# Layer 1's projections for two heads ahead of the heads' small products, exponentials among the raw weights, and the ring of weights one place on

## The chip, the cores and the metric

The kernel runs on one core of a Trainium2 chip. The metric is the device time of one execution in microseconds (us). The core has four engines that matter here: TensorE (PE in the profile, with its weight loads as PEld), VectorE (DVE), ScalarE (ACT) and GpSimd (POOL). SyncE (SP) issues the transfers from HBM. Each engine works through its own list of instructions in order; semaphores tie the lists together.

## The reference

The kernel computes a trunk of two layers over 512 tokens of width 1024, in float32. Layer 0 mixes tokens with four heads of differential attention and four groups of trailing means. Layer 1 is gated linear attention with four heads. Each layer ends with an MLP of width 4096 with squared ReLU. Layer 1, cut to what the change touches:

```python
def _gla_mixer(h, w_in, w_gk_up, b_gk, norm_gain, w_out):     # h is the normed input, chunks of 64 tokens
    proj = h @ w_in                        # q 512, k 512, v 1024, g_out 1024, gk_low 16
    log_a = log_sigmoid(gk_low @ w_gk_up + b_gk) / 16.0        # one decay per token and key channel
    ...
    b = cumsum(gi)                                             # within a chunk
    o_inter = einsum('bhlk,bhkv->bhlv', qi * exp(b), state)
    decay = exp(where(causal, b_i - b_j, -inf))
    attn = einsum('bhijk,bhjk->bhij', qi * decay, ki)
    o_intra = einsum('bhij,bhjv->bhiv', attn, vi)
    new_state = exp(b_last) * state + einsum('bhlk,bhlv->bhkv', ki * exp(b_last - b), vi)
    ...
    o = _rmsnorm(o, norm_gain) * silu(g_out)
    return o @ w_out
```

## The kernel before

Activations lie channel by channel: eight tiles of [128 channels x 512 tokens]. A float32 product is made of three matmuls, since both factors are split into a high and a low part: high weight by high activation (L148), high by low (L149), low by high (L150). A projection into channel-major form (`proj_T`) takes 24 such matmuls into one PSUM bank; a projection into token-major form (`proj_tok`, L172 to L174) takes 96 into four banks at once.

**Banks.** PSUM has eight banks under two names, four "mm" (in the profile `psmm`) for the large products and four "ax" (`psax`) for small products, sums and transposes. A tile takes a name's banks in turn, and waits until the bank's last reader is done.

**Weights.** They arrive in pieces of 1 MB by SP's queue (`load`, L115) into a ring of raw slots (`wraw`), two slots outside the MLPs and five within. Slot k is columns 4Sk to 4S(k+1) of one raw buffer of 24 S columns (S is 512). Each half of a slot is split by ScalarE into the high part (L126, `wh`) and by VectorE into the low part (L127, `wl`), with four tiles each in turn. The very first piece goes in parts straight to slot 0 (`raw0`). Where only two slots are in use, the other columns of the raw buffer serve as spare tiles of 512 columns, `spare(k)`.

**The start.** The norm of a layer is applied after the projection: while PE projects, the squares of x are summed (L246), PE adds them over the partitions (L204 and L205), ScalarE and VectorE form the inverse root, the row `rb` (L216, L217, L209 to L211), and an eviction multiplies a bank by `rb` on its way out (L311 for layer 0's q and k).

**Layer 1.** Head 0's q and k are projected first; then the gates of all four heads run through ScalarE (L697, L698, logarithm L706) and VectorE (subtraction L712, scan L713). `weights(h)` projects a head's q and k (but not head 0's), evicts them (L731 and L735), and makes the head's weights: exponentials of the scans (L722), three transposes (L753), the sums of q·k by chunk (L204, L205), products of 64, 32 and 16 columns (L783), and larger ones (L790), each of them between steps on VectorE and ScalarE. These are called a head's small products here. `values1(i)` projects half of the values in token-major form. `outputs(h)` makes a head's states and outputs (L825, L840, L842), their squares (L844, L848) and the norm of the head (L204, L205, L216, L217, L209). Behind them come the gate projections from `wg1`, Silu on them (L877), and the output projection from `wo1`.

**The order.** The program is written once, and a scheduler at build time orders each engine's list by priority: what is written earlier goes earlier where its inputs allow, `soon()` raises the priority of what stands in it, and `issue_after` holds an instruction behind another. ScalarE holds one set of functions at a time; a change of set is an instruction of its own, ACT_TABLE_LOAD.

Of the kernel before, what the change touches and what calls it, by code (L numbers as in the profile page):

```python
# [13 lines left out]
ALU = mybir.AluOpType  # L14
AX = mybir.AxisListType

P = 128
# [18 lines left out]
def trunk(ctx: ExitStack, tc: tile.TileContext, xT, par, lvl, lam4, wqk0, wu0, wv0, poolw, wo0,  # L36
          wgk, wup, wqk1, wv1, wg1, wo1, w1a, w2a, w1b, w2b, gfin, out):
    nc = tc.nc
    V, A, G, PE = nc.vector, nc.scalar, nc.gpsimd, nc.tensor
# [4 lines left out]
    def T(shape, tag, bufs, dt=F32):  # L44
        cnt[0] += 1
        return sb.tile(shape, dt, tag=tag, bufs=bufs, name=f"{tag}_{cnt[0]}")
# [6 lines left out]
    def turn(name, bufs):  # L53
        ring[name] = ring.get(name, -1) + 1
        return ring[name] % bufs
# [4 lines left out]
    row8 = row16 = tmp2 = row  # L60


    def spare(k):
        return raws[:, k * S:(k + 1) * S]
# [16 lines left out]
    def PS(tag, shape=(P, S)):  # L81
        cnt[0] += 1
        return pp.tile(list(shape), F32, tag=tag, bufs=4, name=f"ps{tag}_{cnt[0]}")

    def small(n, tag="sm"):
        return T([P, n], tag, 24)


    def soon(n=300):
        return tc.high_priority(n)  # L90
# [3 lines left out]
    nc.scalar.dma_start(prm[:, 0:C_ICNT], par[:, 0:C_ICNT])  # L94
    xall = T([P, KB, S], "x", 1)
    x = [xall[:, f, :] for f in range(KB)]
    raw0 = raws[:, 0:4 * S].rearrange("p (a n) -> p a n", a=2)
    xT3 = xT.rearrange("(f p) s -> p f s", p=P)
    for f, nx, nw in ((0, 1, 1), (1, 1, 1), (2, 2, 2), (4, 2, 4), (6, 2, 0)):
# [46 lines left out]
    def mm3(ps, w, a, first, last):  # L146
        (wh, wl), (ah, al) = w, a
        PE.matmul(ps, wh, ah, start=first, stop=False)  # L148
        PE.matmul(ps, wh, al, start=False, stop=False)  # L149
        ended["mm"] = PE.matmul(ps, wl, ah, start=False, stop=last).ins  # L150

    def proj_T(w, act, tag="mm", ps=None, kbs=tuple(range(KB)), first=0, last=KB - 1):

        hi, lo = w
        ps = PS(tag) if ps is None else ps
        for kb in kbs:
            c = slice(kb * P, (kb + 1) * P)
            mm3(ps, (hi[:, c], lo[:, c]), act[kb], kb == first, kb == last)
        return ps
# [106 lines left out]
    act = []  # L266
# [13 lines left out]
    st = Stream(wqk0, 2)  # L280
# [4 lines left out]
    with tc.issue_after(ended["hi"]), tc.issue_after(ended["lo"]), tc.issue_after(ended["mm"]):  # L285
        rb = nrm.rb()
# [19 lines left out]
    def qk_heads(h):  # L306
        for j in range(2):
            ps = (ps0, ps1)[h][j] if h < 2 else proj_T(st.next(), act)
            t = spare(8 + 2 * h + j)
            with soon():  # L310
                V.tensor_tensor(t, ps, rb, ALU.mult)  # L311
            qk[h, j] = t
# [22 lines left out]
    def softmax(h, qt, views, neg):  # L335

        n = (qt + 1) * P
        es, rs, sums, c2 = [], small(2), small(2), small(1)
        for j in range(2):
            e = tmp2()  # L340
            A.activation(e[:, :n], views[j], AF.Exp, bias=neg[:, j:j + 1], scale=0.125, accum_out=sums[:, j:j + 1])
            es.append(e)
        V.reciprocal(rs, sums)
        V.tensor_tensor(c2, rs[:, 1:2], neglam, ALU.mult)
        V.tensor_scalar(out=es[1][:, :n], in0=es[1][:, :n], scalar1=c2, scalar2=None, op0=ALU.mult)
        V.scalar_tensor_tensor(out=es[0][:, :n], in0=es[0][:, :n], scalar=rs[:, 0:1], in1=es[1][:, :n],
                               op0=ALU.mult, op1=ALU.add)
        return es[0]
# [52 lines left out]
    st = Stream(wu0)  # L401
    for i, g in enumerate((3, 2, 1, 0)):
        w = POOL_W[g]
        ps = proj_T(st.next(), act)
# [5 lines left out]
        while step < w:  # L410
# [7 lines left out]
                               op1=ALU.subtract)  # L418
# [234 lines left out]
    act, nrm = add_out(wo0, cat, C_FFN0, NH - 1)  # L653
# [8 lines left out]
    act, nrm = ffn(w1a, w2a, act, nrm, C_MIX1)  # L662
# [4 lines left out]
    st = Stream(wqk1)  # L667
# [11 lines left out]
    with soon():  # L679
        rb = nrm.rb()  # L680
# [6 lines left out]
    qT0, kT0 = row8(), row8()  # L687
# [3 lines left out]
    es, ms, bs = [], [], []  # L691
    for h in range(NH):
# [3 lines left out]
        e, m = tmp(), tmp2()  # L696
# [23 lines left out]
    def expo(out, src):  # L720
        with tc.issue_after(exps):
            last_exp[0] = A.activation(out, src, AF.Exp, scale=GT).ins  # L722

    def weights(h):

        qT, kT = qT0, kT0
        if h:
            ps = proj_T(st.next(), act)
            qT = row8()
            with soon():  # L730
                V.scalar_tensor_tensor(out=qT, in0=ps, scalar=float(P) ** -0.5, in1=rb, op0=ALU.mult, op1=ALU.mult)  # L731
            ps = proj_T(st.next(), act)
            kT = row8()
            with soon():
                V.tensor_tensor(kT, ps, rb, ALU.mult)  # L735
        b = bs[h]
        b3 = b.rearrange("p (c t) -> p c t", t=P)

        e = row16()
        expo(e, b)  # L740
        el = small(NT)
        V.tensor_copy(el, e.rearrange("p (c t) -> p c t", t=P)[:, :, P - 1])
        ebl.append(el)
        V.tensor_tensor(e, e, qT, ALU.mult)
        qeb.append(e)
        d = tmp()
        d3 = d.rearrange("p (c t) -> p c t", t=P)
        V.tensor_tensor(d3, b3[:, :, P - 1:P].to_broadcast([P, NT, P]), b3, ALU.subtract)
        expo(d, d)
        V.tensor_tensor(d, d, kT, ALU.mult)  # L750
        pst = PS("ax")
        for c in range(NT - 1):
            PE.transpose(pst[:, c * P:(c + 1) * P], d[:, c * P:(c + 1) * P], ident)  # L753
        kd = row16(3 * P)
        A.activation(kd, pst[:, 0:3 * P], AF.Copy)
        kdt.append(kd)

        at = row16()
        at3 = at.rearrange("p (c t) -> p c t", t=P)
        attn.append(at)  # L760
        prod = tmp()
        V.tensor_tensor(prod, kT, qT, ALU.mult)
        V.tensor_tensor(at3, col_sums(prod, 0.0).rearrange("p (c t) -> p c t", t=P),
                        lv[:, NLEV:NLEV + 1, :].to_broadcast([P, NT, P]), ALU.mult)
        for l in range(NLEV - 1):
            s = 64 >> l
            nb = S // (2 * s)
            sh = [P, nb, s]
            d = tmp()
            bv, dv, kv, qv = (t.rearrange("p (n t) -> p n t", t=2 * s) for t in (b, d, kT, qT))  # L770
            ref = bv[:, :, s - 1:s].to_broadcast(sh)
            V.tensor_tensor(dv[:, :, 0:s], ref, bv[:, :, 0:s], ALU.subtract)
            V.tensor_tensor(dv[:, :, s:], bv[:, :, s:], ref, ALU.subtract)
            expo(d, d)
            V.tensor_tensor(dv[:, :, 0:s], dv[:, :, 0:s], kv[:, :, 0:s], ALU.mult)
            V.tensor_tensor(dv[:, :, s:], dv[:, :, s:], qv[:, :, s:], ALU.mult)
            psl = PS("ax")
            if s >= 16:

                for p0 in range(0, P, 2 * s):  # L780
                    for c in range(NT):
                        j0 = c * P + p0
                        PE.matmul(psl[p0:p0 + s, c * s:(c + 1) * s], d[:, j0:j0 + s], d[:, j0 + s:j0 + 2 * s],  # L783
                                  start=True, stop=True)
                    A.activation(at3[p0:p0 + s, :, p0 + s:p0 + 2 * s],
                                 psl[p0:p0 + s, 0:NT * s].rearrange("p (c t) -> p c t", t=s), AF.Copy)
                continue
            for c in range(NT):
                cs = slice(c * P, (c + 1) * P)
                PE.matmul(psl[:, cs], d[:, cs], d[:, cs], start=True, stop=True)  # L790
            V.copy_predicated(at3, lv[:, l:l + 1, :].to_broadcast([P, NT, P]),
                              psl.rearrange("p (c t) -> p c t", t=P))

        d = tmp(S // 2)
        bv, kv, qv = (t.rearrange("p (n t) -> p n t", t=2) for t in (b, kT, qT))
        V.tensor_tensor(d, bv[:, :, 1], bv[:, :, 0], ALU.subtract)
        expo(d, d)
        V.tensor_tensor(d, d, kv[:, :, 0], ALU.mult)
        V.tensor_tensor(d, d, qv[:, :, 1], ALU.mult)
        pair = [P, NT, P // 2, 2]  # L800
        V.copy_predicated(at.rearrange("p (c n t) -> p c n t", c=NT, t=2),
                          lv[:, NLEV - 1:NLEV, :].rearrange("p a (n t) -> p a n t", t=2).to_broadcast(pair),
                          col_sums(d, 0.0).rearrange("p (c n t) -> p c n t", c=NT, t=1).to_broadcast(pair))
# [5 lines left out]
    def values1(half):  # L809
        for t, ps in enumerate(proj_tok(vst, act)):  # L810
            vt = spare(12 + 4 * half + t)
            with soon():
                A.activation(vt, ps, AF.Copy, scale=r1[:, t:t + 1])
            vv[t][half] = vt
# [39 lines left out]
            ot.append(o)  # L854


    for h in range(3):
        weights(h)
    values1(0)
    weights(3)  # L860
    outputs(0)
    outputs(1)
    values1(1)
    outputs(2)
    outputs(3)

    st = Stream(wg1)
    gts = []
    for f in range(KB):
        ps = proj_T(st.next(), act)  # L870
# [12 lines left out]
    act, nrm = add_out(wo1, oh, C_FFN1, KB - 1)  # L883
# [86 lines left out]
```

## Time and profile before

| | |
|---|---|
| median of 3 runs | 1117.22 us (1116.67 to 1118.0) |
| profiled execution | 1116.72 us |
| its span (first to last instruction) | 1114.8 us |
| mean granted clock of TensorE | 0.983 |
| TensorE busy | 1078.9 us, 97% |
| VectorE busy | 827.7 us, 74% |
| ScalarE busy | 532.4 us, 48% |
| moved from HBM | 100.59 MB |

A row of the timeline gives the start, the duration, engine, line, operation, output <- inputs, and in brackets how long the engine had been idle and what released it. A row of the windows gives the stretch, its length, the busy time and number of instructions of PE, PEld, DVE, ACT and POOL, the granted clock of PE, the busy share of DMA and GB/s. A row of the page's groups gives a count, the total busy time and the mean of one in ns, then the idle time ahead of it. Line numbers are those of the kernel before; in the changed one they are higher by 1 from the new `turn` on and by up to 9 towards the end.

### The profile page before, as it was taken

To read this page: it belongs to the slowest core of one execution; us is meant where nothing else is said; L and a number is where in the kernel's file an instruction comes from. 1 tells how busy PE (TensorE), PEld (TensorE's weight loads), DVE (VectorE), ACT (ScalarE), POOL (GpSimd) and SP (SyncE) were. 2 spreads that over 40 slices of the span, in tenths; PEclk is the share of its full clock that TensorE was granted. 3 is DMA by queue.
4 is the path that set the end of the run, shared out by engine and by line. 5 is a ranking of instruction groups with operands and counts; after the bars stand their busy time and mean duration, and the time that the engine had idled before them with its cause. 6 is when DMAs were issued, how large, how long until landed. Compare 5 with 4: busy or idle time off the path is not lost.

```text
span 1114.8 us, 12893 instructions
## 1 busy us (share of the span) xinstructions
PE 1078.9 (97%) x4968; PEld 869.2 (78%) x4968; DVE 827.7 (74%) x1234; ACT 532.4 (48%) x885; POOL 2.3 (0%) x20
## 2 busy tenths in 40 slices
PE   7999969999999999999969999999999999999996
PEld 5676748888888888888757778888888888888885
DVE  6757667696497597598888877655697596696696
ACT  6444525455454453454554546544553443453453
POOL 0000000000000000000000000000000000000000
PEclk9999979999999999999979999999999999999999
DMA  7132123214304305203220222342305305206102
GB/s 239 73 113 82 71 85 124 85 38 151 118 34 170 130 4 189 76 17 114 76 76 1 76 76 77 113 151 86 123 1 189 113 1 195 108 1 223 41 1 76
DMA packets 17917, 103.52 MB, mean 93 GB/s; under 512 B 2016, under 2 KB 3040, under 8 KB 6208
## 3 DMA queue, kind: packets, MB, share of 16 engines
q1 hardware_dynamic: 17712, 102.67, 25.6%
q8 instruction: 39, 0.64, 0.2%
q14 instruction: 22, 0.18, 0.1%
q10 hardware_dynamic: 144, 0.03, 0.0%
HBM read 100.59 MB, written 2.10 MB: 92 GB/s over the span
## 4 chain that ended last, share of the span: by engine, by line
PE 92%; DVE 4%; ACT 2%; DMA 1%; issue 1%; SPq 0%; DVEq 0%
PE psmm L148 14%; PE psmm L149 14%; PE psmm L150 14%; PE psmm L566 6%; PE psmm L565 6%; PE psmm L567 6%; PE psax L148 3%; PE psax L150 3%; PE psax L149 3%; PE psax L567 3%; PE psax L565 3%; PE psax L566 3%; PE psmm L174 2%; PE psmm L173 2%; PE psmm L172 2%; PE psax L325 1%
## 5 line engine op out<-in xcount | busy, mean ns | idle before, releaser
L126 ACT ACTIVATE wh<-wraw 128x1024 fp32r<-128x1024 f32 x230 | 243.5, 1061 | 403.0 <-PE psmm L149 161.6
L127 DVE TENSOR_TENSOR wl<-wraw,wh 128x1024 fp32r<-128x1024 f32 x230 | 280.8, 1222 | 64.8 <-ACT wh L126 63.9
L148 PE MATMUL psmm<-row,wh 128*128 128x512 f32 x736 | 290.6, 396 | 15.3 <-DVE wraw L408 7.2
L149 PE MATMUL psmm<-row,wh 128*128 128x512 f32 x736 | 291.1, 396 | 0.4 <-DVE row L187 0.4
L150 PE MATMUL psmm<-row,wl 128*128 128x512 f32 x736 | 290.4, 395 | 0.0
L148 PEld LDWEIGHTS psmm<-row,wh 128*128 128x128 f32 x736 | 139.2, 189 | 48.7 <-DVE wraw L408 7.8
L149 PEld LDWEIGHTS psmm<-row,wh 128*128 128x128 f32 x736 | 139.4, 189 | 32.6 <-issue 3.1
L150 PEld LDWEIGHTS psmm<-row,wl 128*128 128x128 f32 x736 | 139.3, 189 | 31.2 <-issue 2.6
L565 PE MATMUL psmm<-wh,row 128*128 128x512 f32 x320 | 124.6, 390 | 0.0
L567 PE MATMUL psmm<-wl,row 128*128 128x512 f32 x320 | 124.6, 389 | 0.0
L566 PE MATMUL psmm<-wh,row 128*128 128x512 f32 x320 | 124.6, 389 | 0.0
L540 DVE TENSOR_TENSOR wraw<-wraw 128x1024 f32<-128x1024 f32 x64 | 77.4, 1222 | 0.3
L492 DVE TENSOR_TENSOR row<-row,row 128x512 fp32r<-128x512 f32 x112 | 75.1, 685 | 0.3 <-ACT row L491 0.3
L567 PEld LDWEIGHTS psmm<-wl,row 128*128 128x128 f32 x320 | 60.1, 188 | 12.5
L566 PEld LDWEIGHTS psmm<-wh,row 128*128 128x128 f32 x320 | 60.1, 188 | 12.4
L565 PEld LDWEIGHTS psmm<-wh,row 128*128 128x128 f32 x320 | 60.1, 188 | 12.4
L491 ACT ACTIVATE row<-row 128x512 fp32r<-128x512 f32 x112 | 65.7, 618 | 5.3 <-DVE row L518 5.3
L506 DVE SCALAR_TENSOR_TENSOR tmp<-psmm,rb 128x512 f32<-128x512 f32 x48 | 33.0, 687 | 45.7 <-PE psmm L150 45.7
L511 ACT ACTIVATE row<-tmp 128x256 f32<-128x256 f32 x128 | 45.9, 406 | 11.0 <-DVE tmp L506 10.7
L150 PE MATMUL psax<-row,wl 128*128 128x512 f32 x128 | 49.8, 389 | 0.0
L567 PE MATMUL psax<-wl,row 128*128 128x512 f32 x128 | 49.8, 389 | 0.0
L149 PE MATMUL psax<-row,wh 128*128 128x512 f32 x128 | 49.8, 389 | 0.0
(233 smaller groups left out, 1316.5 us busy)
## 6 DMA issues: line engine op xcount, KB each, us to landing
wraw<-in_w1a SPq DMA_DIRECT2D x16, 1024.0 KB, 4.8
wraw<-in_w2a SPq DMA_DIRECT2D x16, 1024.0 KB, 4.8
wraw<-in_w1b SPq DMA_DIRECT2D x16, 1024.0 KB, 4.8
wraw<-in_w2b SPq DMA_DIRECT2D x16, 1024.0 KB, 4.8
wraw<-in_wo SPq DMA_DIRECT2D x8, 1024.0 KB, 4.7
wraw<-in_wqk SPq DMA_DIRECT2D x7, 1024.0 KB, 4.8
wraw<-in_wv SPq DMA_DIRECT2D x6, 1024.0 KB, 4.8
wraw<-in_wg SPq DMA_DIRECT2D x4, 1024.0 KB, 4.7
```

The lines of the kernel that those rows point to most:

```text
L126: ended["hi"] = A.activation(hi, src, AF.Copy).ins
L127: ended["lo"] = V.tensor_tensor(lo, src, hi.bitcast(F32), ALU.subtract).ins
L148: PE.matmul(ps, wh, ah, start=first, stop=False)
L149: PE.matmul(ps, wh, al, start=False, stop=False)
L150: ended["mm"] = PE.matmul(ps, wl, ah, start=False, stop=last).ins
L491: A.activation(hi, src, AF.Copy)
L492: V.tensor_tensor(lo, src, hi.bitcast(F32), ALU.subtract)
L511: A.activation(raw[name][:, j, :], r[:, th * 256:th * 256 + 256], AF.Square)
L540: V.tensor_tensor(out[k], in0[k], in1[k], ALU.subtract)
L565: PE.matmul(ps[t], hi, wh[:, cs], start=f, stop=False, skip_group_check=True)
L566: PE.matmul(ps[t], lo, wh[:, cs], start=False, stop=False, skip_group_check=True)
L567: PE.matmul(ps[t], hi, wl[:, cs], start=False, stop=l, skip_group_check=True)
```

## The change

There are three edits. First, the ring of raw slots is turned one place on ahead of the first load, so that the second piece of `wqk0` goes to slot 1 and not to slot 0, in which `raw0` lies. Every later piece outside the MLPs lies in the other slot of the two. Second, layer 0's q and k tiles use four spare tiles in turn (8 to 11), and the softmax's exponentials `e`, which came from the pool of rows, now use four others (12 to 15). Third, in layer 1 q and k of a head are projected by a function of its own, `project()`, which is called for heads 1 and 2 before `weights(0)`; the calls that follow are values, weights and projections in turn, and the four outputs come last.

```diff
     x = [xall[:, f, :] for f in range(KB)]
+    turn("raw", 2)
     raw0 = raws[:, 0:4 * S].rearrange("p (a n) -> p a n", a=2)
...
-            t = spare(8 + 2 * h + j)
+            t = spare(8 + 2 * (h % 2) + j)
...
-            e = tmp2()
+            e = spare(12 + turn("es", 4))
             A.activation(e[:, :n], views[j], AF.Exp, bias=neg[:, j:j + 1], scale=0.125, accum_out=sums[:, j:j + 1])
...
+    qks = [(qT0, kT0)]
+
+    def project():
+
+        ps = proj_T(st.next(), act)
+        qT, kT = row8(), row8()
+        with soon():
+            V.scalar_tensor_tensor(out=qT, in0=ps, scalar=float(P) ** -0.5, in1=rb, op0=ALU.mult, op1=ALU.mult)
+        ps = proj_T(st.next(), act)
+        with soon():
+            V.tensor_tensor(kT, ps, rb, ALU.mult)
+        qks.append((qT, kT))
+
     def weights(h):
 
-        qT, kT = qT0, kT0
-        if h:
-            ps = proj_T(st.next(), act)
-            qT = row8()
-            with soon():
-                V.scalar_tensor_tensor(out=qT, in0=ps, scalar=float(P) ** -0.5, in1=rb, op0=ALU.mult, op1=ALU.mult)
-            ps = proj_T(st.next(), act)
-            kT = row8()
-            with soon():
-                V.tensor_tensor(kT, ps, rb, ALU.mult)
+        qT, kT = qks[h]
...
-    for h in range(3):
-        weights(h)
+    project()
+    project()
+    weights(0)
     values1(0)
+    weights(1)
+    project()
+    weights(2)
+    values1(1)
     weights(3)
     outputs(0)
     outputs(1)
-    values1(1)
     outputs(2)
     outputs(3)
```

The lists of instructions move at three places. The first is SP's queue at the start, from the last of the first small transfers on (`in_par` are parameters, `in_lam` a small vector of the attention). Before:

```order
L103 DMA par_62<-in_par 128x192
L115 DMA wraw_61<-in_wv 128x2048
L115 DMA wraw_61<-in_wqk 128x2048
L292 DMA tmp_282<-in_lam 128x256
L115 DMA wraw_61<-in_wv 128x2048
L115 DMA wraw_61<-in_wqk 128x2048 x2
```

Now:

```order
L104 DMA par_62<-in_par 128x192
L116 DMA wraw_61<-in_wqk 128x2048
L116 DMA wraw_61<-in_wv 128x2048 x2
L293 DMA tmp_282<-in_lam 128x256
L116 DMA wraw_61<-in_wqk 128x2048 x2
```

The load of `wqk` stands first, and the first load of `wv` behind it.

The second place is VectorE in layer 1, from the last scans of the gates (L713, now L714) to the start of head 0's chain. Before, and here 29 instructions of head 0's chain and one correction of its sums lie between the two pieces:

```order
L713 SCALAR_TENSOR_TENSOR row_4279<-row_3999,row_4256 128x512
L713 SCALAR_TENSOR_TENSOR row_4282<-row_3999,row_4263 128x512
L748 TENSOR_TENSOR tmp_4297<-row_4273 128x512
L742 COPY sm_4294<-row_4292 128x4
L127 TENSOR_TENSOR wl_4874<-wraw_61,wh_4873 128x1024
L744 TENSOR_TENSOR row_4292<-row_4292,row_4235 128x512
```

```order
L798 TENSOR_TENSOR tmp_4410<-tmp_4410,row_4236 128x256
L799 TENSOR_TENSOR tmp_4410<-tmp_4410,row_4235 128x256
L791 COPY_PREDICATED row_4307<-lvl_1586,psax_4392 128x512
L731 SCALAR_TENSOR_TENSOR row_4453<-psmm_4428,rb_4216 128x512
L735 TENSOR_TENSOR row_4484<-psmm_4459,rb_4216 128x512
```

Now:

```order
L714 SCALAR_TENSOR_TENSOR row_4241<-row_3967,row_4210 128x512
L128 TENSOR_TENSOR wl_4580<-wraw_61,wh_4579 128x1024
L714 SCALAR_TENSOR_TENSOR row_4244<-row_3967,row_4217 128x512
L713 TENSOR_TENSOR row_4224<-row_4224,tmp_4223 128x512
L713 TENSOR_TENSOR row_4231<-row_4231,row_4230 128x512
L714 SCALAR_TENSOR_TENSOR row_4247<-row_3967,row_4224 128x512
L714 SCALAR_TENSOR_TENSOR row_4250<-row_3967,row_4231 128x512
L732 SCALAR_TENSOR_TENSOR row_4290<-psmm_4265,rb_4184 128x512
L735 TENSOR_TENSOR row_4291<-psmm_4297,rb_4184 128x512
L732 SCALAR_TENSOR_TENSOR row_4353<-psmm_4328,rb_4184 128x512
L735 TENSOR_TENSOR row_4354<-psmm_4360,rb_4184 128x512
L753 TENSOR_TENSOR tmp_4391<-row_4241 128x512
```

The four evictions of the projections (L732 and L735) stand right behind the scans, and a weight split (L128) among the scans. On ScalarE, the weight splits move in the same way: the one of `wh_4550` stands ahead of the gates' second and third exponential, and the one of `wh_4579` between the second and third logarithm. On PE, the last matmul of head 2's k projection had head 0's transposes (L753) right behind it; now 23 matmuls of the value projection stand between the two.

The third place is ScalarE at the outputs: Silu (L877, now L886), the inverse root of a head's norm (L216 and L217, now L217 and L218), and squares of outputs (L844, L848, now L849, L853). Before:

```order
L216 ACTIVATE tmp_5383<-psax_5384 128x512
L217 ACTIVATE tmp_5383<-tmp_5383 128x512
L844 ACTIVATE tmp_5416<-psax_5408 128x512
L848 ACTIVATE row_5418<-psax_5408,par_62 128x512
L844 ACTIVATE row_5428<-psax_5420 128x512
L848 ACTIVATE row_5430<-psax_5420,par_62 128x512
L126 ACTIVATE wh_5572<-wraw_61 128x1024
L202 ACTIVATE row_5435<-tmp_5416 128x512
L877 ACT_TABLE_LOAD
L877 ACTIVATE wraw_61<-wraw_61 128x512
L216 ACT_TABLE_LOAD
L216 ACTIVATE tmp_5433<-psax_5434 128x512
```

Now:

```order
L886 ACT_TABLE_LOAD
L886 ACTIVATE wraw_61<-wraw_61 128x512
L849 ACTIVATE row_5296<-psax_5288 128x512
L853 ACTIVATE row_5298<-psax_5288,par_62 128x512
L127 ACTIVATE wh_5601<-wraw_61 128x1024
L886 ACTIVATE wraw_61<-wraw_61 128x512
L203 ACTIVATE row_5303<-tmp_5284 128x512
L886 ACTIVATE wraw_61<-wraw_61 128x512
L217 ACT_TABLE_LOAD
L217 ACTIVATE tmp_5301<-psax_5302 128x512
L218 ACT_TABLE_LOAD
L218 ACTIVATE tmp_5301<-tmp_5301 128x512
```

Silu was met first behind the third output's norm; now it is met ahead of it, and the table is changed before each following norm. ScalarE's list had 8 ACT_TABLE_LOADs and now has 13.

## The prediction

> **What bounds the kernel now.** I read the page's span, its busy shares and the chain of waits first, then the waits of PE, then PE in stretches of time, then the timeline where a stretch is not full.
>
> ```profile
> span 1114.8 us, 12893 instructions
> PE 1078.9 (97%) x4968; PEld 869.2 (78%) x4968; DVE 827.7 (74%) x1234; ACT 532.4 (48%) x885; POOL 2.3 (0%) x20
> PE 92%; DVE 4%; ACT 2%; DMA 1%; issue 1%; SPq 0%; DVEq 0%
> ```
>
> PE is busy for 97% of the span and carries 92% of the chain that ends last, so only a place where PE waits, or runs at a lower clock, can give time back. Such places are few:
>
> ```profile
> 0.00:20.00 20.00, 14.08 (x48) 9.60 (x48) 12.85 (x27) 13.49 (x28) 0.40 (x7) 1.00 0.82 273
> 20.00:40.00 20.00, 18.17 (x75) 13.69 (x76) 15.05 (x32) 8.28 (x13) 0.00 (x0) 0.91 0.34 115
> 40.00:140.00 100.00, 99.17 (x418) 69.21 (x416) 65.63 (x173) 50.22 (x137) 0.56 (x5) 1.00 0.24 83
> 140.00:160.00 20.00, 11.65 (x30) 6.89 (x31) 13.46 (x26) 4.85 (x8) 0.67 (x6) 0.66 0.31 118
> 160.00:560.00 400.00, 399.78 (x1775) 329.49 (x1775) 304.28 (x375) 191.64 (x281) 0.64 (x2) 1.00 0.26 92
> 560.00:580.00 20.00, 12.10 (x60) 8.93 (x59) 18.44 (x33) 10.71 (x18) 0.00 (x0) 0.80 0.29 106
> 580.00:600.00 20.00, 17.61 (x111) 14.50 (x110) 15.00 (x36) 6.54 (x15) 0.00 (x0) 0.77 0.00 1
> 600.00:760.00 160.00, 160.00 (x917) 129.95 (x916) 115.97 (x203) 86.00 (x139) 0.00 (x0) 1.00 0.25 91
> ```
>
> The first pair of numbers is the stretch and PE's busy time in it; the third number from the end is the granted clock. PE is full from 160 to 560 and from 600 to 760, and all but full from 40 to 140. It is short, and its clock is below 1.00, at the start, at 140 to 160 (layer 0's pooling heads) and at 560 to 600, where layer 1 begins. The change touches the first and the last; in the middle one the order of VectorE around L408 and L417 is unchanged, so I let that loss stand.
>
> **Part 1: the ring of weights, at the start.** Before, the second load of `wqk` goes to the slot that the first one still fills; with the ring one place on it finds a free slot.
>
> ```profile
> 6.84 0.74 SPq L115 DMA_DIRECT2D wraw<-in_wv  x1
> 15.14 0.33 SPq L115 DMA_DIRECT2D wraw<-in_wqk  x1
> 19.98 2.01 ACT L126 ACTIVATE wh<-wraw 128x1024 fp32r<-128x1024 f32 x2 [2.51 <-DMA wraw<-in_wqk]
> 21.09 0.50 PE L148 MATMUL psmm<-row,wh 128*128 128x512 f32 x1 [1.88 <-ACT wh L126]
> 24.84 0.63 PE L149 MATMUL psmm<-row,wh 128*128 128x512 f32 x1
> 25.26 0.63 PE L150 MATMUL psmm<-row,wl 128*128 128x512 f32 x1
> 27.18 0.40 PE L148 MATMUL psmm<-row,wh 128*128 128x512 f32 x1
> 27.41 0.39 PE L149 MATMUL psmm<-row,wh 128*128 128x512 f32 x1
> 29.24 0.39 PE L204 MATMUL psax<-row,onesr 128*128 128x512 f32 x1
> 34.53 2.48 DVE L311 TENSOR_TENSOR wraw<-psmm,rb 128x512 f32<-128x512 f32 x4
> 35.36 0.47 PE L172 MATMUL psmm<-wh,row 128*128 128x512 f32 x1 [0.52 <-DVE wraw L311]
> ```
>
> The load now issues where `wv` did, at 6.84 instead of 15.14, about 8 us earlier, so its split no longer waits 2.51 for DMA. PE loses 1.88 us of waiting, and after it a spell of low clock (a matmul starts every 0.42 at 24.84 and every 0.23 at 27.41), together about 3.4 us at L204. But what PE does next needs the norm's row `rb`, and VectorE and ScalarE now put weight splits ahead of that norm (two L128, 1.22 each, stand before the last two sums of squares, and one more before the correction). The splits' durations are these rows of the page:
>
> ```profile
> L126 ACT ACTIVATE wh<-wraw 128x1024 fp32r<-128x1024 f32 x230 | 243.5, 1061 | 403.0 <-PE psmm L149 161.6
> L127 DVE TENSOR_TENSOR wl<-wraw,wh 128x1024 fp32r<-128x1024 f32 x230 | 280.8, 1222 | 64.8 <-ACT wh L126 63.9
> ```
>
> PE, unhindered, reaches L204 at 29.24 − 3.4 = 25.8. From L204 to L311 it was 34.53 − 29.24 = 5.3; one more split of 1.06 now stands inside that chain on ScalarE, of which I count 0.7, since another part of the chain gives a split up. So L311 comes at 31.8 and L172 0.83 later, as before, at 32.6 instead of 35.36: 2.8, of which I take **2.6 us gained**. Bounds: 3.4 if the norm keeps up, 1 if the early load takes DMA time from the rows of x that share the first 20 us (0.82 busy). The exponentials in the raw columns take four tiles in turn where the pool gave any; a ring of four can make ScalarE wait for PE's transposes. PE has no gap from 40 to 139, ScalarE is half busy there (50.22 of 100), and the exps stay interleaved with the transposes in the order: 0, from −1 to +1.
>
> **Part 2: layer 1's projections first.** This is the main term.
>
> ```profile
> 565.44 2.33 DVE L713 TENSOR_TENSOR_SCAN row<-row,row 128x512 f32<-128x512 f32 x2
> 567.84 0.39 PE L150 MATMUL psmm<-row,wl 128*128 128x512 f32 x1
> 570.91 0.52 PE L753 MATMUL psax<-par,tmp 128*128 128x128 f32 x3 [2.68 <-DVE tmp L750]
> 573.22 0.79 PE L204 MATMUL psax<-tmp,onesr 128*128 128x512 f32 x1 [1.79 <-ACT tmp L202]
> 588.96 0.67 DVE L731 SCALAR_TENSOR_TENSOR row<-psmm,rb 128x512 f32<-128x512 f32 x1
> 589.69 0.50 PE L172 MATMUL psmm<-wh,row 128*128 128x512 f32 x1
> 594.05 0.49 PE L753 MATMUL psax<-par,row 128*128 128x128 f32 x3
> 617.30 0.49 PE L753 MATMUL psax<-par,tmp 128*128 128x128 f32 x3
> ```
>
> PE ends the q and k projections of heads 1 and 2 at 567.84 + 0.39 = 568.23. They fill all four "mm" banks, and VectorE empties the first of them only at 588.96, behind the whole chain of head 0's small products. The value projection (L172), which needs such a bank, starts at 589.69. For 21.5 us PE has only head 0's small products (L753, L204, L783, L790), each waiting for the one before through VectorE and ScalarE. What are these products worth where other work covers them? From 594.05 to 617.30 PE does head 1's, with 68 value matmuls among them: 23.25 − 68 × 0.23 = 7.6 us. So 21.5 − 7.6 = **13.9 us** are lost there, to waiting and low clock.
>
> After, VectorE empties all four banks straight behind the scans, and PE has 23 value matmuls (5.3 us) ahead of head 0's first transposes and the rest of them between its products. What is late next is the scans themselves. On ScalarE, the third and fourth logarithm of the gates (L706, now L707) stand behind a weight split which reuses the tile of head 2's q projection, so it cannot run before PE ends that, 24 × 0.23 before 568.23, at 562.7. Another split, brought ahead of the gates' exponentials (L698, now L699), waits likewise for head 1's k projection, and one more split of 1.22 enters between the scans on VectorE. The last pair of scans ended at 565.44 + 2.33 = 567.8. I take 2.0 for ScalarE's waits and 1.2 for VectorE's split: 571.0. The first eviction (0.67) ends at 571.7, and PE waits from 568.23 to there: **3.5 us lost**. Bounds: 1.5 (only the inserted 1.22 counts, and the scans' own end) and 5 (both ScalarE's waits in full).
>
> A wait of this length has been followed by low clock: after 1.88 at 21.09 seven or so matmuls took 0.42 instead of 0.23, and L204 at 573.22 took 0.79 instead of 0.39. I take **1.5 us lost**, from 0 to 2.3. The Trainium skill ("TensorE: Matmul & The Clock Gate", Part 1: The HAM clock gate) puts the ramp at about 3.4 us of time at half rate, in a free-running window; by that the term would be at most 1.7 and its size would change from one run to the next. The slow spell at the start, about 3 us, agrees.
>
> Head 0's transposes come about 6 us after they did, but 5.3 us of matmuls stand before them and some 70 among the products, so I allow **0.8 us** of short waits there. Heads 1 to 3 have their projections (48 matmuls) or values (96) around them, as heads 1 to 3 had before, when PE was full.
>
> **Part 3: the outputs.** With heads and values shuffled, the gate projections fall before and between the four outputs, and ScalarE meets Silu among the outputs' rsqrt. The order shows 13 table loads where it had 8.
>
> ```profile
> 695.12 1.28 ACT L877 ACT_TABLE_LOAD   x1
> 696.41 0.63 ACT L877 ACTIVATE wraw<-wraw 128x512 f32<-128x512 f32 x1
> 697.06 1.28 ACT L216 ACT_TABLE_LOAD   x1
> 698.36 0.60 ACT L216 ACTIVATE tmp<-psax 128x512 f32<-128x512 f32 x1
> 700.27 0.63 ACT L217 ACTIVATE tmp<-tmp 128x512 f32<-128x512 f32 x1
> 700.93 0.69 DVE L209 SCALAR_TENSOR_TENSOR row<-psax,tmp 128x512 f32<-128x512 f32 x1 [3.16 <-ACT tmp L217]
> ```
>
> Five more cost 5 × 1.28 = 6.4 us of ScalarE, which is 48% busy. It reaches PE only where an output's products wait for an "ax" bank that the previous output still holds, with little gate work between: 21 gate matmuls (4.8 us) stand between the second and third outputs, 11 (2.5 us) between the third and fourth. An output's chain with its two table loads is 1.28 + 0.60 + 1.28 + 0.63 + 0.69 = 4.5 us. So the third is covered, and the fourth lacks about 2: I take **2.5 us lost** in all, from 0 to 4. The last gate matmuls, 117 × 0.23 = 27 us behind the last output, cover the final Silus and products.
>
> The Trainium skill ("ScalarE: Activation LUTs", What ACT_TABLE_LOAD costs) speaks against this part: it gives 1283 ns for the load and 1380 ns of drain for every switch, and so 13.3 us for the five. The rows show the first and not the second: 695.12 + 1.28 is 696.40 and the Silu starts at 696.41, and the next load follows that Silu's end (697.04) at 697.06. I stay with 1.28.
>
> **The sum**, against the profiled execution's 1116.72 (span 1114.8, so 1.9 lies around it; the median of the runs is 1117.22, 0.5 above): −2.6 − 13.9 + 3.5 + 1.5 + 0.8 + 2.5 = −8.2, and 1116.7 − 8.2 = **1108.5 us**.
>
> **Rivals.** (a) All covered: the splits wait for nothing, the scans end as before, and neither clock nor outputs cost anything. The gain is 2.6 + 13.9 less the 1.5 of the inserted split: 15.0, time 1101.7. For it: PE was full from 600 to 760 with the same chains. Against it: the split behind q's tile is a real dependence.
> (b) Slower: the switches of table set expose the chain. If each of outputs two, three and four makes PE wait its whole 4.5 us, 13.4 us are lost in place of 2.5, and the time is 1116.7 − 8.2 − 2.5 + 13.4 = 1119.4. It decides from (8.2 + 2.5) / 3 = 3.6 us a head on. For it: two loads and a Silu now stand in such a chain, and more Silus queue with the gates. Against it: gate matmuls stand between, and before, PE was full where two of these chains ran (600 to 760). By the skill's figure of 2.66 a switch, the chain would be 7.2 us a head; the rows above don't bear it out.
> (c) The stall only moves: the gate chain ends so late that PE stands still, or waits between head 0's products, for some 8 us more, the 13.9 come back whole, and the time is 1116.7 − 2.6 + 2.5 = 1116.6. For it: VectorE is 18.44 of 20 busy at 560 to 580, so whatever goes first there delays the rest by as much. Against it: PE needs of VectorE only four evictions (2.7 us) to start 96 matmuls.
>
> **How the numbers follow.** The forecast has a chance of 0.65, with 1103.5 to 1112.5 as its own range (its bounds, not all at one end at once); (a) 0.17; (b) 0.08; (c) and mixtures with it 0.10. The range from 1101.5 to 1114.5 leaves out (b), (c) and half of the tail of (a). Two runs of this kernel differ by about 0.1%, and less than 0.2% (2.2 us) would be no change. Faster by more: the forecast, (a) and a third of (c), 0.86. Same: most of the rest of (c), 0.06. Slower: (b), 0.08.
>
> **What would show it.** Right: L172's first matmul of the second load's group near 32 to 33; at 560 to 600 PE's busy time rises from 29.7 of 40 to over 35, with one wait of 2 to 5 us on VectorE's evictions (L732 or L735) and no string of waits on L758 to L795; 13 table loads, with a few short waits of PE at the outputs. Wrong: waits at L829 or L844 of 3 us and more for each output (b); a new wait of 10 us before the first value matmul (c); a wait on the exponentials' tiles in layer 0, which I put at nothing; a stretch from 160 to 540 that isn't shorter by the start's 2.6 alone.

## The result and the profile after

The changed kernel takes **1107.02 us** in the median of 4 runs (1106.55 to 1107.57), beside 1116.95 for the kernel before in runs of the same time: a ratio of 0.9912, with a 95% interval from 0.9895 to 0.9929, some 9.9 us. In a later comparison on one chip it took 1107.09 and the kernel before 1117.04, ratio 0.9915 (0.9901 to 0.9928). The profiled execution of the changed kernel took 1106.55, with a span of 1104.8.

The page after: PE is still busy for 97% of a shorter span, and ScalarE has five instructions more, the table loads.

```profile
span 1104.8 us, 12896 instructions
PE 1073.0 (97%) x4968; PEld 863.6 (78%) x4968; DVE 826.9 (75%) x1234; ACT 538.3 (49%) x890; POOL 2.3 (0%) x20
PE 91%; DVE 4%; ACT 3%; issue 1%; DMA 1%; SPq 0%; DVEq 0%
```

The stretches that answer to those of before, moved on with the work (columns as before, the clock third from the end):

```profile
20.00:40.00 20.00, 18.49 (x86) 14.10 (x85) 17.68 (x42) 7.97 (x18) 0.00 (x0) 1.00 0.47 165
137.00:160.00 23.00, 15.20 (x44) 8.85 (x45) 15.94 (x29) 5.61 (x9) 0.67 (x6) 0.70 0.24 97
555.00:575.00 20.00, 17.05 (x70) 13.69 (x69) 16.29 (x22) 10.24 (x15) 0.00 (x0) 0.91 0.30 106
575.00:600.00 25.00, 25.00 (x165) 19.58 (x164) 19.70 (x42) 13.95 (x26) 0.00 (x0) 1.00 0.13 43
700.00:760.00 60.00, 58.79 (x260) 48.26 (x259) 40.46 (x55) 33.09 (x44) 0.00 (x0) 1.00 0.40 147
```

The start runs at full clock. Where layer 1 begins, 3 us of 45 are lost and a little clock, where before 10 of 40 were lost and a fifth of the clock. From 700 to 760, where PE had been full, it now lacks 1.2 us. PE's waits after say the same (two at the very start, for the first weights, and one of 0.2 are left out):

```profile
PE psmm L149 <- DVE wraw L409: 7.2, 1, 7.2
PE psmm L173 <- DVE row L732: 3.0, 1, 3.0
PE psmm L149 <- ACT row L187: 2.1, 1, 2.1
PE psax L205 <- ACT row L203: 1.8, 2, 1.2
PE psmm L173 <- ACT wh L127: 0.9, 1, 0.9
PE psax L354 <- DVE wraw L347: 0.7, 2, 0.4
PE psmm L151 <- DVE wl L128: 0.6, 1, 0.6
```

The string of waits between head 0's small products (L753, L783, L790 and L204 of the prediction's fences) is gone. In its place stands one wait of 3.0 us on the first eviction, L732.

Where the 10 us came from is read off three marks. The first is the first value matmul of layer 0, at 35.36 before. The second is the first eviction in layer 1. The third is the last matmul of the program, of which before

```profile
549.35 0.69 DVE L684 TENSOR_TENSOR row<-psmm,rb 96x512 f32<-96x512 f32 x1
1105.96 0.39 PE L567 MATMUL psmm<-wl,row 128*128 128x512 f32 x1
```

and after, with the first mark ahead of them:

```profile
32.51 0.47 PE L173 MATMUL psmm<-wh,row 128*128 128x512 f32 x1 [0.93 <-ACT wh L127]
546.23 0.69 DVE L685 TENSOR_TENSOR row<-psmm,rb 96x512 f32<-96x512 f32 x1
1095.08 0.39 PE L568 MATMUL psmm<-wl,row 128*128 128x512 f32 x1
```

The marks moved by 2.85, 3.1 and 10.9 us. So 2.85 come from the start, 0.3 from layer 0's stretch, and 7.75 from the second mark to the last matmul: what is gained where layer 1 begins, less what the outputs cost. (The span is shorter by only 10.0, not 10.9: behind the last matmul it takes 9.7 us to the end where it took 8.8. VectorE's last instruction ends 5.9 us behind that matmul in both, so the difference lies behind it, where only the last store to HBM is left. Why that takes longer is not known.)

### The profile page after: what moved, and what is told of

It reads as the page before. It is cut to its first block, busy times and chain, and to the rows that moved or that the text cites. A ratio compares the mean times of both kernels' runs of the same rounds, so it can differ in the third digit from the quotient of the medians.

```text
span 1104.8 us, 12896 instructions
## 1 busy us (share of the span) xinstructions
PE 1073.0 (97%) x4968; PEld 863.6 (78%) x4968; DVE 826.9 (75%) x1234; ACT 538.3 (49%) x890; POOL 2.3 (0%) x20
## 3 DMA queue, kind: packets, MB, share of 16 engines
q1 hardware_dynamic: 17712, 102.67, 25.8%
## 4 chain that ended last, share of the span: by engine, by line
PE 91%; DVE 4%; ACT 3%; issue 1%; DMA 1%; SPq 0%; DVEq 0%
PE psmm L149 14%; PE psmm L150 14%; PE psmm L151 14%; PE psmm L568 6%; PE psmm L567 6%; PE psmm L566 6%; PE psax L150 3%; PE psax L151 3%; PE psax L149 3%; PE psax L567 3%; PE psax L568 3%; PE psax L566 3%; PE psmm L173 2%; PE psmm L174 2%; PE psmm L175 2%; PE psax L326 1%
## 5 line engine op out<-in xcount | busy, mean ns | idle before, releaser
L127 ACT ACTIVATE wh<-wraw 128x1024 fp32r<-128x1024 f32 x230 | 243.5, 1061 | 402.6 <-PE psmm L150 161.1
L128 DVE TENSOR_TENSOR wl<-wraw,wh 128x1024 fp32r<-128x1024 f32 x230 | 280.8, 1222 | 70.9 <-ACT wh L127 69.9
```

What stands on the lines that cost most here:

```text
L127: ended["hi"] = A.activation(hi, src, AF.Copy).ins
L128: ended["lo"] = V.tensor_tensor(lo, src, hi.bitcast(F32), ALU.subtract).ins
```

## The experiments

Eleven kernels were run beside the kernel before, each ratio being to runs of that kernel made in the same comparison. "Layer 1 on" is the time from the first eviction of layer 1 to the last matmul in the run's profile, the second and third mark above. It leaves the start out, whose length differs by more than a microsecond from one profile to the next: with the ring turned, the first value matmul starts between 31.7 and 33.1. A second profile of the changed kernel gives 549.0, 0.2 from the first. The three kernels with layer 1 as before differ by 1.3 in it; the clock has a part in that, as the last section shows.

| kernel | median us | ratio to before (95%) | layer 1 on |
|---|---|---|---|
| before | 1116.95 | 1 | 556.6 |
| changed | 1107.02 | 0.9912 (0.9895 to 0.9929) | 548.9 |
| ring alone | 1113.95 | 0.9976 (0.9966 to 0.9986) | 557.6 |
| tiles alone | 1117.38 | 1.0000 (0.9990 to 1.0009) | 557.9 |
| order alone | 1107.57 | 0.9915 (0.9899 to 0.9932) | 549.1 |
| ring and order | 1106.11 | 0.9905 (0.9892 to 0.9919) | 549.0 |
| two evictions ahead of the scans | 1105.05 | 0.9897 (0.9882 to 0.9912) | 546.6 |
| splits held behind the gates | 1104.37 | 0.9891 (0.9876 to 0.9905) | 545.8 |
| Silu held | 1106.31 | 0.9905 (0.9889 to 0.9922) | 547.7 |
| projections first, later calls as before | 1102.38 | 0.9869 (0.9854 to 0.9884) | 545.3 |
| the same, Silu held | 1100.45 | 0.9858 (0.9843 to 0.9873) | 542.9 |
| the same, Silu held, no fixed tiles | 1100.03 | 0.9852 (0.9838 to 0.9867) | 542.9 |

### The three edits by themselves

The ring alone, on the kernel before:

```diff
+    turn("raw", 2)
     raw0 = raws[:, 0:4 * S].rearrange("p (a n) -> p a n", a=2)
```

> The kernel before with the first edit alone, the ring of raw slots one place on. If the start's gain is the slot that is free, and nothing later gives it back: the first value matmul of layer 0 starts near 32.5 us instead of 35.36, all later stretches only move, head 0's small products in layer 1 still stand alone for 21 us, and the time is 3 us below before, about 1114. If the earlier loads collide with something later, or the gain is swallowed by the wait before the pooling heads: within 1 us of before.

1113.95 us. The first value matmul starts at 32.35, and head 0's small products wait as before:

```profile
32.35 0.47 PE L173 MATMUL psmm<-wh,row 128*128 128x512 f32 x1 [0.93 <-ACT wh L127]
...
PE psax L754 <- DVE tmp L751: 2.7, 1, 2.7
PE psax L784 <- DVE row L777: 1.9, 1, 1.9
PE psax L791 <- DVE tmp L777: 1.8, 1, 1.8
```

(The first row is of the timeline, the others of PE's waits.) The free slot is worth the start's 3 us, and nothing takes them back.

The tiles alone, on the kernel before:

```diff
-            t = spare(8 + 2 * h + j)
+            t = spare(8 + 2 * (h % 2) + j)
...
-            e = tmp2()
+            e = spare(12 + turn("es", 4))
```

> The kernel before with the second edit alone, q, k and the exponentials in fixed tiles of the raw buffer. If these tiles are only room: the time of before, 1117 within 1 us, and PE's waits of before. If four tiles in turn hold ScalarE up: a few waits of PE on the transposes between 40 and 137 us, 1 to 2 us slower.

1117.38 us, no change within 0.1%. The waits between 40 and 137 us are there, but they are 0.3 us in all:

```profile
PE psmm L148 <- ACT row L186: 2.1, 1, 2.1
PE psax L353 <- DVE wraw L346: 0.3, 1, 0.3
```

The wait on L186 was 0.6 before. It is ScalarE's row of the last attention head, right ahead of the stall of 7.2 on L408: in VectorE's order a weight split (L127) now stands one place ahead of that head's last product (L377). The head's chain on VectorE began 0.9 us earlier against the start, the stall keeps its length, and its end comes only 0.1 us later, 115.2 us behind the first value matmul where it was 115.1.

The order alone, which is the changed kernel without its first two edits:

```diff
-    turn("raw", 2)
...
-            t = spare(8 + 2 * (h % 2) + j)
+            t = spare(8 + 2 * h + j)
...
-            e = spare(12 + turn("es", 4))
+            e = tmp2()
```

> The changed kernel without its first two edits: layer 1's new order of calls alone. If the main term is the four banks emptied before head 0's chain: the start as before (first value matmul near 35.4), the 21 us of head 0 alone gone, one wait of about 3 us on the first eviction, and 6.8 us below before, about 1110. If the new order needs the tiles that the second edit frees, or the other slots: waits of PE in layer 1 that the changed kernel does not have, and less than 4 us gained.

1107.57 us, 9.3 under before, where 6.8 was expected. Its profile shows the single wait, 2.9 on L731, and "layer 1 on" as in the changed kernel, within 0.2. So the order needs neither of the other edits. But the single gains, 3.0 and 9.3, are more than the 9.9 of all together.

So the tiles were taken out of the changed kernel, on one chip with the changed kernel itself:

```diff
-            t = spare(8 + 2 * (h % 2) + j)
+            t = spare(8 + 2 * h + j)
...
-            e = spare(12 + turn("es", 4))
+            e = tmp2()
```

> The changed kernel without its second edit (q, k and exponentials in fixed tiles). With those tiles, PE's wait ahead of the last attention sums (on ScalarE's L187) was 2.1 us in three kernels, without them 0.6 in three, and VectorE's eviction after it came about 0.5 us later against the start. If that is the tiles' price: 0.5 to 1 us less than the changed kernel, 1106.2. If the tiles cost nothing and the gains of the single edits do not add for another reason: the changed kernel's time, 1107.0, within 0.3.

> The changed kernel itself, beside the others on the same chip: 1107.0.

1106.11 (1105.68 to 1106.72) beside 1107.09 (1107.02 to 1107.70): a microsecond less, with the runs apart. PE's wait shrinks as expected:

```profile
PE psmm L149 <- ACT row L187: 0.6, 1, 0.6
PE psmm L150 <- DVE row L188: 0.4, 1, 0.4
```

With the fixed tiles the changed kernel is about 1 us slower. In the profiles of these two, 0.5 of it lies in layer 0, up to the end of the stall (115.6 us behind the first value matmul, and 115.1 without the tiles), "layer 1 on" is 549.0 in both, and 0.7 lies behind the last matmul. That last part isn't shown to be the tiles' price: two other kernels with these tiles (the projections first, with and without Silu held) don't have it. Even so, ring and order gain 10.9 together and 12.3 by themselves. These 1.4 us weren't found. Runs of the kernel before lie between 1114.7 and 1118.2, so it may be no more than scatter of the runs compared.

### The wait of 3 us on the first eviction

The prediction put it down to weight splits of the values, brought among the gates' steps, which make the scans and so the evictions late. In the first test, these splits are held: ScalarE's behind the gates' logarithms, VectorE's behind the last scan.

```diff
+            src = self.raw[:, h, :]
+            if self.hold is not None and self.n > 1:
+                hi, lo = w_tiles(src.shape[-1])
+                with soon(), tc.issue_after(self.hold[0]):
+                    A.activation(hi, src, AF.Copy)
+                with soon(), tc.issue_after(self.hold[1]):
+                    V.tensor_tensor(lo, src, hi.bitcast(F32), ALU.subtract)
+                return hi, lo
+            return split_w(src)
...
     vst = Stream(wv1)
+    vst.hold = (exps, scanned)
```

> The changed kernel with the later splits of the first value weights held: ScalarE's behind the gates' logarithms, VectorE's behind the last scan. If it is these splits, put among the gates, that make the evictions late: the scans end some 3 us earlier, close to the end of head 2's k projection, the wait of 3.0 us shrinks to under 0.5, the clock stays up, and the time is about 4 us less, 1103. If the scans are late for another reason, or if the splits are now late for the value matmuls: less than 1 us gained.

1104.37 us. First the rows of the changed kernel, whose ScalarE splits a weight ahead of the gates' exponentials (554.02) and another between the logarithms (L707), and whose VectorE splits between the scans (L714):

```profile
554.02 1.06 ACT L127 ACTIVATE wh<-wraw 128x1024 fp32r<-128x1024 f32 x1 [0.24 <-PE psmm L150]
...
559.21 0.62 ACT L707 ACTIVATE row<-row 128x512 f32<-128x512 f32 x1
559.73 1.05 ACT L127 ACTIVATE wh<-wraw 128x1024 fp32r<-128x1024 f32 x1
561.68 1.20 DVE L128 TENSOR_TENSOR wl<-wraw,wh 128x1024 fp32r<-128x1024 f32 x1
565.12 2.33 DVE L714 TENSOR_TENSOR_SCAN row<-row,row 128x512 f32<-128x512 f32 x2
568.09 0.80 PE L173 MATMUL psmm<-wh,row 128*128 128x512 f32 x1 [2.95 <-DVE row L732]
```

and then those of the kernel with the splits held:

```profile
562.65 2.33 DVE L722 TENSOR_TENSOR_SCAN row<-row,row 128x512 f32<-128x512 f32 x2
565.62 0.50 PE L181 MATMUL psmm<-wh,row 128*128 128x512 f32 x1 [0.52 <-DVE row L740]
572.97 0.52 PE L766 MATMUL psax<-par,tmp 128*128 128x128 f32 x3 [0.71 <-DVE tmp L763]
```

Both kernels start layer 1 at the same 546.2. The last scans start 2.5 us earlier, the wait falls from 2.95 to 0.52, and "layer 1 on" falls by 3.1. The splits among the gates were the cause of all but the last 0.5. A part is given back at head 0's first transposes (0.71), since the splits now stand ahead of its chain on VectorE, and the time is 1.4 above the 1103 that was expected.

In the second test, head 1's projection is written ahead of the scans, and its two evictions stand in front of them on VectorE, which was idle there; the splits stay. (`project()` moves up for this, and returns its last eviction.)

```diff
+    evicted = project()
     for e, m in zip(es, ms):
         b = row16()
         with tc.issue_after(evicted):
...
-    project()
     project()
     weights(0)
```

> The changed kernel, with head 1's projection written ahead of the gates' scans and its two evictions in front of the scans on VectorE, where VectorE had 1.9 us idle; head 2's two evictions stay behind the scans. If the wait of 3.0 us on the first eviction is a wait for a bank: the value matmuls of the first two banks (12, 2.7 us) run during the scans' end, the wait falls under 0.5 us, PE's clock does not fall (another 1.4 us), and the time is about 4 us under the changed kernel's, 1103. If PE waits there for the values' split weights or for something else: the wait stays, 1107.

1105.05 us, where 1103 was expected. The wait is gone altogether: PE has two banks for its first value matmuls while the scans end. But the scans are as late as they were, and so is head 0's chain, which PE now reaches sooner:

```profile
573.44 0.52 PE L760 MATMUL psax<-par,tmp 128*128 128x128 f32 x3 [1.53 <-DVE tmp L757]
```

Of the 3.0 us of waiting and 1.5 of low clock, 1.5 came back here and 0.3 behind it (L797). "Layer 1 on" shows 2.3 us gained and the median 2.0, half of what was expected. (The profiled execution, the slowest of its four, reached layer 1 1.8 us later than the changed kernel's, 0.4 of it at the first value matmul and the rest in layer 0, where the clock was low for 17.1 us at the pooling heads and not for 13.7.) The value weights are split when they were, at the same places among the gates, and yet the wait is gone: PE had waited for a bank, and not for weights.

### The table loads among the outputs

```diff
-        A.activation(r, r, AF.Exp, scale=-0.5)
+        ended["rs"] = A.activation(r, r, AF.Exp, scale=-0.5).ins
...
+    last_rs = ended["rs"]
     st = Stream(wg1)
...
-    with tc.issue_after(last_exp[0]):
+    with tc.issue_after(last_exp[0]), tc.issue_after(last_rs):
         for f in range(KB):
             last = A.activation(gts[f], gts[f], AF.Silu)
```

> The changed kernel with Silu held behind the norms of all four heads, so that ScalarE changes its table once to Silu and once back. Table loads 5 instead of 13. If the table loads among the outputs are what the last output waits for: the wait of 1.2 us at the fourth head's sums goes, and the time is about 1 us less, 1106. If the Silus are then late for the output projection: a wait at its first matmuls, no gain or a loss.

1106.31 us, 0.7 under the changed kernel, with overlapping runs; "layer 1 on" falls by 1.1. ScalarE's table loads in the changed kernel and, in the second fence, in this one:

```profile
L886 ACT ACT_TABLE_LOAD x3 | 3.8, 1283 | 0.1
L217 ACT ACT_TABLE_LOAD x3 | 3.8, 1283 | 0.1
L218 ACT ACT_TABLE_LOAD x3 | 3.8, 1283 | 0.1
```

```profile
L887 ACT ACT_TABLE_LOAD x1 | 1.3, 1283 | 0.0
L890 ACT ACT_TABLE_LOAD x1 | 1.3, 1283 | 0.0
```

From 700 to 760 PE is full again (60.00 of 60). A wait of 1.0 on L203 stays; it is in layer 0, near 139 us. So the eight loads more that the changed kernel has, some 10 us of ScalarE, had cost PE about 1 us.

### Only the projections first

The changed kernel moves two things in layer 1: the projections go first, and the calls behind them are dealt out anew. Here the projections go first and the later calls stand as before.

```diff
     project()
     project()
     weights(0)
-    values1(0)
     weights(1)
-    project()
     weights(2)
-    values1(1)
+    values1(0)
+    project()
     weights(3)
     outputs(0)
     outputs(1)
+    values1(1)
     outputs(2)
     outputs(3)
```

> The changed kernel with the two projections first, but the later calls in the order of before (weights of heads 0, 1 and 2, then the values, head 3, two outputs, the other values, two outputs). If emptying the banks first is the whole gain: as the changed kernel, about 1107. If the covering work must also be dealt out among the heads: VectorE needs some 21 us for each head's chain, heads 0 to 2 then have 96 value matmuls (22 us) and their own 23 us of small products against 60, PE waits between the small products again, and the time is 1111 or more.

1102.38 us: faster than the changed kernel by 4.6, where 1111 or more was expected if the covering work had to be dealt out. That expectation was wrong. PE has no gap over the heads' products, and VectorE is nearly full but not quite:

```profile
555.00:580.00 25.00, 24.00 (x136) 18.17 (x134) 23.67 (x45) 14.35 (x24) 0.00 (x0) 1.00 0.24 85
600.00:650.00 50.00, 50.00 (x367) 37.99 (x363) 43.22 (x95) 28.50 (x58) 0.00 (x0) 1.00 0.18 64
650.00:700.00 50.00, 47.73 (x274) 40.54 (x272) 36.03 (x58) 34.63 (x47) 0.00 (x0) 1.00 0.21 71
```

The scheduler still puts many value matmuls among head 0's products, and since the values are called later, it leaves behind the gates the split that stood between their logarithms, and VectorE's behind the scans. PE's waits where layer 1 begins are small, and the larger ones at the outputs:

```profile
PE psax L205 <- ACT row L203: 3.1, 3, 1.3
PE psax L758 <- DVE tmp L755: 0.8, 1, 0.8
PE psmm L173 <- DVE row L732: 0.2, 1, 0.2
```

The wait on L732 is 0.2 instead of 3.0, and the clock does not fall (1.00). The two are worth 2.8 and 1.5 us. Against them stand 0.8 at L758 and, of L203's three waits, two at the outputs of 1.3 and 1.0 where the changed kernel has one of 1.2. That makes 2.4 us net. "Layer 1 on" is shorter by 3.5, so about 1 us isn't explained by these rows. The rest lies outside: the profiled executions differ by 5.1, with 0.8 at the start, which is written alike in both, and 0.8 behind the last matmul.

With Silu held as above:

> The kernel with the projections first and the later calls as before, and with Silu held behind the norms. It waited 2.3 us in two places for the third and fourth heads' sums, behind table loads. If these loads are the cause: both waits go, 1100.5. If they only cover another wait (VectorE's states and squares): the waits stay as they are, 1102.

1100.45 us, as expected. PE is full from 650 to 700 (50.00 of 50); the 1.0 left on L203 is that of layer 0. Without the fixed tiles as well:

> The projections first, the later calls as before, Silu held behind the norms, and no fixed tiles for q, k and exponentials. If the tiles cost 0.5 to 1 us: 1099.7. If not: 1100.45, as with the tiles.

1100.03 us (1099.26 to 1101.67), 0.4 less, within the scatter of its runs. "Layer 1 on" is the same 542.9. These two kernels beat the changed one by 6.6 and 7.0 us: the intervals, 0.9843 to 0.9873 and 0.9838 to 0.9867, lie clear of its 0.9895 to 0.9929.

## Why the prediction was right

It gave 1108.5 us, in a range from 1101.5 to 1114.5, and the kernel took 1107.02. Term by term, against the profiles:

- **The start, 2.6 gained.** Measured 2.85 at the first value matmul (3.0 in the ring alone), and no clock lost from 20 to 40. What ends the chain is as put, the norm's row and not PE: L205 starts at 25.98 (25.8 predicted) and L312 at 31.67 (31.8).
- **The tiles in layer 0, 0, from −1 to +1.** About 1 us lost beside the kernel without them, of which the profiles put 0.5 in layer 0, and hardly where it was looked for. PE's waits on the transposes, which the prediction named as a sign of being wrong, are there, but small (0.3 with the tiles alone, 0.7 in the changed kernel); with them a split changed places ahead of the stall at the pooling heads.
- **Head 0's products alone, 13.9.** This can't be read by itself. With the new wait of 2.95, the low clock of 1.5 and the 1.2 at the outputs, the 7.75 gained from layer 1 on give 13.4. That is a remainder and no measurement of its own, and beside the ring alone or the tiles alone, whose "layer 1 on" is longer, it would be 1.0 or 1.3 more.
- **The new wait, 3.5 lost.** Measured 2.95. The mechanism is shown by the kernel with the splits held. Of its two parts, the wait of ScalarE for PE's tile hardly counted: the first of the moved splits waited 0.24 and the second not at all, at 559.73, where the prediction had it stand until 562.7. So the step with "cannot run before PE ends that" was wrong, and with it the real dependence that was held against rival (a): the tile was free earlier. The time went to the splits themselves, two of 1.06 on ScalarE ahead of the logarithms' end and one of 1.20 among the scans.
- **Low clock, 1.5 lost.** Seven matmuls, from 568.09 to 571.19, took 3.1 us where 7 × 0.23 is 1.6: 1.5. The clock fell after this wait, and did not where the wait was 0.5. Read in steps of 0.1 us, the granted clock is 0.50 from 567.7 to 571.1, 3.4 us, and the first 0.4 of it is still the wait. In the order alone it fell later, 0.7 behind the end of the wait, and the loss by the same count (3.4 us at half rate, all of it with matmuls) is 1.7; so that it was 1.5 here is in part luck. The Trainium skill ("TensorE: Matmul & The Clock Gate", Part 1: The HAM clock gate) gives about 3.4 us for the ramp, and these traces agree.
- **Short waits at head 0, 0.8 lost.** None was seen in the changed kernel. They appear, 0.7 to 1.5, once the wait ahead of them is taken away.
- **The outputs, 2.5 lost.** Measured 1.2, at the fourth head's sums (L205), where it was put, and 1.1 came back with Silu held. The table loads took 1283 ns each, and among the outputs the next instruction followed within 0.03 us, but for one that waited 0.8 us for PE. So the further 1380 ns of drain in the Trainium skill ("ScalarE: Activation LUTs", What ACT_TABLE_LOAD costs) are not seen in these rows either. The rule of the Trainium skill to batch activation calls by set ("ScalarE: Activation LUTs", Table sets: the hidden batching unit) is borne out: holding Silu was worth 0.7 us of the median in the changed kernel, within the scatter of its runs, and 1.9 with the later calls as before.

So the sum was 8.2 and the measured gain 9.9 (10.0 in the spans). The losses at the outputs and the short waits were put 2.1 too high and the new wait 0.5 too high, and the start and layer 0's stretch gave 0.5 more; against that stand 0.5 less at head 0's products and 0.9 behind the last matmul, which no term had. The path is the one that was forecast; that the sum came within 1.8 us is in part luck, since these errors offset each other. Rival (a) was half right, since most of what it called covered was covered. Rival (b) had the right place, but one head of three waited, and for 1.2 us and not 4.5. Gate matmuls stood between; that these covered the others is argued, not tested. Rival (c) did not happen in the changed kernel; the run with two evictions ahead of the scans shows its shape, a wait that comes back in part behind the next product.

One step that went unseen cost most: the prediction priced the third edit as one, and did not ask whether the later calls had to be dealt out anew. With the projections first and the later calls left alone, the edits gained 14.5 us. The new order of calls takes back 4.6 of them, of which 3.5 are seen in "layer 1 on"; most of these come from the splits that it pulls among the gates, as the kernel with the splits held shows (3.1).

## What to carry to other kernels

When a large engine stands idle beside a chain of small steps, ask first which buffer its next work needs, and on which engine's list the release of that buffer stands: here four short evictions at the wrong place in VectorE's list were worth more than 10 us. When work is called earlier, everything that it needs comes earlier too, and a scheduler may put those steps (here weight splits) into a chain that others wait for; hold them explicitly, or call the work later: the one gave 2.7 us here, the other 4.6. Test the parts of such a change separately, also when the whole is a gain: here one part took back a third of what the other brought.

## What the runs showed of the hardware

The granted clock of TensorE fell to 0.50 after waits of 1.9 to 3 us in these profiles, and did not fall after waits of 0.5 or 0.9, nor after one of 1.2 (the changed kernel, 700 to 760) or of 1.5 (two evictions ahead of the scans, 1.00 from 560 to 580). So a wait of 3 us costs about 4.5, and taking away the larger part of it takes away the clock's share as well.

Read in steps of 0.1 us, from 15 to 45, 135 to 165 and 540 to 605, the spells at 0.50 are 3.4, 10.2, 13.7, 17.1 or 20.5 us long in all these profiles, that is, one, three, four, five or six times 3.41. Here are the spells in layer 1 of the changed kernel, of the kernel before, and of the ring alone, without their first and last tenth:

```profile
567.80:571.10 3.30, 3.01 (x7) 2.46 (x8) 3.30 (x7) 0.00 (x0) 0.00 (x0) 0.50 0.00 0
572.10:589.10 17.00, 10.05 (x79) 8.13 (x80) 12.48 (x33) 7.09 (x17) 0.00 (x0) 0.50 0.17 62
567.10:587.40 20.30, 12.89 (x90) 10.28 (x89) 15.77 (x39) 7.58 (x18) 0.00 (x0) 0.50 0.15 52
```

The last two kernels have the same layer 1, with nearly the same waits, and yet one spell is 3.4 us longer than the other; its "layer 1 on" is 1.0 longer. In the tiles alone the spell is 20.5 us as well, and "layer 1 on" 1.3 longer. So a microsecond of a profile can hang on how many of these steps the clock stays low, and differences of that size between single profiles should not be put down to an edit unless a wait of that size goes with them.
